# mLSTM denominators and the moments of the first norm: blocks are added on VectorE and then summed over partitions by one product each

## The chip, the core and the metric

One core of a Trainium2 chip. Its engines work side by side, each through its own list of instructions in order, and wait for one another by semaphores: TensorE (matrix products, "PE" in the profile, its loads of the stationary operand "PEld"), VectorE ("DVE"), ScalarE ("ACT"), GpSimd ("POOL") and SyncE ("SP"), which issues most transfers. The metric is device time of one execution in microseconds (us). Of the kernel before there are three timed runs: 2336.39, 2336.71 and 2338.29 us, median 2336.71.

## The reference

One inference step of a one-layer hybrid decoder for two groups of tokens: 256 tokens of a new sequence ("prompt") and 8 sequences of 8 new tokens that bring a state ("sample"), 320 tokens together. All is float32. Two mixers read one projection of the layer's input, an mLSTM with 4 heads and an HGRN2 with 8; their outputs are merged, projected, normalised, and a feed-forward block with a second norm follows. Two places matter here. The first is the mLSTM's denominator:

```python
d = jnp.exp(logd - m_t[..., None])
w_inter = jnp.exp(inter - m_t)
s = jnp.einsum('bhtk,bhsk->bhts', qc, kc) * d
num = jnp.einsum('bhts,bhsv->bhtv', s, vc) + w_inter[..., None] * jnp.einsum('bhtk,bhkv->bhtv', qc, C)
den = jnp.sum(s, axis=-1) + w_inter * jnp.einsum('bhtk,bhk->bht', qc, n)
h = num / jnp.maximum(jnp.abs(den), jnp.exp(-m_t))[..., None]
```

The second is the first of the two layer norms:

```python
x1 = _layernorm(DEEPNORM_ALPHA * x + mix, ln1_g, ln1_b)      # mean and variance over 2048 channels
hid = jnp.square(jax.nn.relu(jnp.einsum('btd,df->btf', x1, w_up)))
y = _layernorm(DEEPNORM_ALPHA * x1 + jnp.einsum('btf,fd->btd', hid, w_down), ln2_g, ln2_b)
```

## The kernel before

**The main stream.** Activations lie with channels on the partitions and the 320 tokens along a row. Every large projection is cut into 304 tiles of 128 output channels; a tile runs over 16 blocks of 128 input channels. To keep float32 accuracy at the faster float32r format, both operands are split into a high part and the rest, and each block takes three products (a "triple"): high x high, high x low, low x high. They are issued by `run_main` through the helper `mm` (L327), so that almost all products have line 327. In the profile a tile's bank is `bank`, the split weights are `wh`/`wl` (later also parts of `bb`), the split activations `xh`/`xl` (later `ra`, `rxb`, `bb`). Weights arrive by DMA into `wr`; `prep` splits half a tile at a time: ScalarE copies the high part (helper `A`, L321), VectorE subtracts (L469).

**Order.** The order on every engine is fixed when the program is built. `Sched` keeps a modelled clock for each engine and a list of chains (Python generators), each of which yields its next instruction with a cost. After every triple `pump` lets the chains issue what the model takes to be ready; a product of a chain goes into TensorE's stream between two triples, at the earliest 450 ns after the model has its inputs finished. `acq` and `rel` take and give back buffers and PSUM banks, `post` and `wait` are events between chains. On the chip semaphores hold an instruction back until its inputs are really there, and all that is behind it on its engine waits too.

**mLSTM, per head h.** `m_E` makes the decay factors in the tile `E` (512 columns, shown as `f`): columns 0 to 127 hold source block 0 against target block 0 of the prompt, 128 to 255 source block 0 against target block 1, 256 to 383 source block 1 against target block 1, and 384 to 511 the sample tokens (rows 64 to 127; the other rows and the columns between are zero). `m_S` multiplies the scores of queries and keys in (L859, L860), so that `E` holds `s`, and splits it into `sh`, `sl` (L868) and the sample's `ss` (L869). `m_num` computes the prompt's outputs. Its denominators, column sums of `E`, come first: three products of a 128 x 128 block of `E`, as the stationary operand, with a column of ones (`one`, in the tile `misc`), so each of them is one column wide. Target block 1 takes two of them, added up in PSUM. Then come the numerators (512 columns wide), and `ln_post` and `rsqrt` for the head's norm on VectorE and ScalarE (L974 to L995). `m_sample` does the sample: eight products with the old states `C` (tiles `f` and `rx`), two of `ss` with `vs`, and the denominator: the column sum of `E[:, 384:512]` and of the two halves of `qn`, which holds the query times the old normaliser, again with `one`, three products into one PSUM column. L1101 copies it to SBUF. All of that is issued between the triples of the main stream while the head's neighbours and the merge gates are projected; `sigmoid` (L1209 to L1216) turns the gates.

**Layer norm.** `ev_wo` (first norm) and `ev_dn` (second) add the residual to each of the 16 blocks `z` of 128 channels. `ln_sum` keeps two running sums on VectorE, S1 of z (L1678) and S2 of its square (L1679; the square on ScalarE), for the tiles up to 14. Then `ln_pre` multiplies S1 and S2 with a 128 x 128 block of ones (`ones`), which sums over partitions and spreads the sum to all of them; the products are 320 columns wide and stay open in PSUM. When the last block arrives, `ln_final` adds two more products, of z and of its square, to the same banks, and the statistics follow on ScalarE and VectorE (L1705 to L1713). After the first norm the products with `w_up` don't wait for the statistics; they run on z scaled by the norm's gain (`zg`, L1754), and `ev_up` applies the statistics behind them.

Of the kernel before, what the change touches and what calls it, by code (L numbers as in the profile page):

```python
# [13 lines left out]
ALU = mybir.AluOpType  # L14
# [6 lines left out]
TOK = 320  # L21
# [201 lines left out]
def wait(*evs):  # L223
    return ("wait", evs)


def acq(pool, n=1):
    return ("acq", pool, n)
# [6 lines left out]
def post(ev):  # L235
    return ("set", ev)


def act(n, psum=False, ptr=0):
    return ((61 if psum else 112) + n) / 1.2 + 93 * ptr  # L240
# [6 lines left out]
def pe_f(n, m=128):  # L247
    return max(212.0 if m == 128 else 162.0, n * 1.66)
# [35 lines left out]
class Program:  # L284
# [561 lines left out]
    def m_S(self, h):  # L846
        v, m = self.nc.vector, self.mh[h]
        if h:
            yield wait(self.mh[h - 1]["S"])
        yield wait(*m["q"], *m["k"], m["E"])  # L850
        b = yield acq(self.sbank)
        qk = m["qk"]
        for lo, n, ks, qs in ((0, 256, 0, lambda c: qk[:, c, 0:256]), (256, 128, 128, lambda c: qk[:, c, 128:256]),
                              (384, 64, 192, lambda c: by_row(qk[:, c, :], 256, False))):
            for c in range(2):
                yield ("pe", pe_f(n), lambda: self.mm(
                    b[:, lo:lo + n], qk[:, 2 + c, ks:ks + 128], qs(c), start=c == 0, stop=c == 1))
        E, Es = m["eb"], m["Es"]
        yield ("dve", dve(384, True), lambda: v.tensor_tensor(E[:, 0:384], b[:, 0:384], E[:, 0:384], ALU.mult))  # L859
        yield ("dve", dve(64, True), lambda: v.tensor_tensor(Es, b[64:128, 384:448].rearrange("p (x r) -> p x r", x=4), Es, ALU.mult))  # L860
        yield rel(self.sbank, b)
        shl = yield acq(self.shl)
        m["shl"] = shl
        sh, sl, ss = shl
        f = lambda x: x.bitcast(F32)
        yield ("act", act(384), lambda: self.A(sh, E[:, 0:384]))
        yield ("act", act(128), lambda: self.A(ss[64:128, 0:128], E[64:128, 384:512]))
        yield ("dve", dve(384), lambda: v.tensor_tensor(sl, E[:, 0:384], f(sh), ALU.subtract))  # L868
        yield ("dve", dve(128), lambda: v.tensor_tensor(ss[64:128, 128:256], E[64:128, 384:512], f(ss[64:128, 0:128]), ALU.subtract))  # L869
        yield ("act", act(256), lambda: self.A(ss[0:64], f(ss[64:128])))  # L870
        yield post(m["S"])

    def m_V(self, h):
# [123 lines left out]
    def m_num(self, h):  # L997
        v, m = self.nc.vector, self.mh[h]
        if h:
            yield wait(self.mh[h - 1]["N"])  # L1000
        yield wait(m["S"], m["Vt"])
        hb = yield acq(self.hb)
        m["hb"] = hb
        E = m["eb"]
        sh, sl, ss = m["shl"]
        vh, vl = m["vhl"][:, 0], m["vhl"][:, 1]
        db = yield acq(self.sbank)
        m["db"] = db
        one = self.one
        yield ("pe", 212, lambda: self.mm(db[:, 0:1], E[:, 0:128], one, start=True, stop=True))  # L1010
        yield ("pe", 212, lambda: self.mm(db[:, 1:2], E[:, 128:256], one, start=True, stop=False))
        yield ("pe", 212, lambda: self.mm(db[:, 1:2], E[:, 256:384], one, start=False, stop=True))
        for i in range(2):
            b = yield acq(self.sbank)
            jobs = [(c, s) for c, s in (((0, 0),), ((128, 0), (256, 1)))[i]]
            n = 0
            for c, s in jobs:
                for x, w in ((sh, vh), (sh, vl), (sl, vh)):
                    st, sp = n == 0, n == 3 * len(jobs) - 1
                    yield ("pe", pe_r(512), lambda: self.mm(b, x[:, c:c + 128], w[:, s, :], start=st, stop=sp))  # L1020
                    n += 1
            yield from self.ln_post(h, i, b, db[:, i:i + 1], hb[:, i, :], 128, True)
            yield rel(self.sbank, b)
        yield rel(self.sbank, db)
        yield post(m["N"])
# [40 lines left out]
    def m_sample(self, h):  # L1066
        nc, v, m = self.nc, self.nc.vector, self.mh[h]
        if h:
            yield wait(self.mh[h - 1]["QW"])
        yield wait(*m["q"], m["bc_"], self.rows_ev)  # L1070
        qk, bc = m["qk"], m["bc"]

        qz = yield acq(self.qz)
        qn = yield acq(self.qn)
        for c in range(2):
            qc = cap(qz, 256 * c, [[136, 2], [32, 4], [1, 8]])
            yield ("dve", dve(64), lambda: v.tensor_tensor(qc, by_token(qk[:, c, :], 256, False), by_token(bc, 640, False), ALU.mult))
            n4 = cap(self.n0[:, h, c, :], 0, [[4, 2], [1, 4], [0, 8]])
            yield ("dve", dve(64), lambda: v.tensor_tensor(by_token(qn, 128 * c, True), qc, n4, ALU.mult))
        yield post(m["QW"])  # L1080
        nb = yield acq(self.sbank)
        for k in range(2):
            yield wait(*m["parts"][8 * k:8 * k + 8])
            cbs = m["cbs"][8 * k:8 * k + 8]
            yield ("pe", PE_C, lambda: [self.mm(
                nb[32 * x:32 * x + 32, :], qz[:, 256 * c + 128 * k + 32 * x:256 * c + 128 * k + 32 * x + 32], cbs[4 * c + x],
                start=k == 0 and c == 0, stop=False, skip_group_check=True) for c in range(2) for x in range(4)])
            for c in range(2):
                self.s.spawn(self.m_update(h, 8 * k + 4 * c, cbs[4 * c:4 * c + 4]), 3)
        yield rel(self.qz, qz)  # L1090
        yield wait(m["S"], m["Vt"])
        E = m["eb"]
        ss = m["shl"][2]
        for i in range(2):
            yield ("pe", pe_r(512), lambda: self.mm(nb, ss[:, 128 * i:128 * i + 128], m["vs"], start=False, stop=i == 1, skip_group_check=True))
        db = yield acq(self.sbank)
        yield ("pe", 212, lambda: self.mm(db[:, 0:1], E[:, 384:512], self.one, start=True, stop=False))
        for c in range(2):
            yield ("pe", 212, lambda: self.mm(db[:, 0:1], qn[:, 128 * c:128 * c + 128], self.one, start=False, stop=c == 1))
        dn = yield acq(self.sm)  # L1100
        yield ("dve", 80, lambda: v.tensor_copy(dn[:, 0:1], db[:, 0:1]))  # L1101
        yield rel(self.sbank, db)
        yield rel(self.qn, qn)
        yield post(m["S0"])
        yield wait(m["N"])
        hb = m["hb"]
        yield from self.ln_post(h, 2, nb, dn[:, 0:1], hb[:, 2, :], 128, True)
        yield rel(self.sbank, nb)
        yield rel(self.sm, dn)
        for j in range(4):  # L1110
            b = yield acq(self.sbank)
            for i in range(3):
                yield ("pe", PE_T, lambda: nc.tensor.transpose(b[:, 128 * i:128 * i + 128], hb[:, i, 128 * j:128 * j + 128], self.ident))  # L1113
            jj = 4 * h + j
            o = yield acq(self.tst)
            g = self.vec[:, V_MLG + jj:V_MLG + jj + 1]
            yield ("act", act(NP_, True, 1), lambda: self.A(o[:, 0:NP_], b[:, 0:NP_], scale=g))
            yield ("act", act(64, True, 1), lambda: self.A(by_row(o, NP_, False), by_row(b, NP_, True), scale=g))
            yield rel(self.sbank, b)
            yield ("sp", 620, lambda: self.dma(self.hT[jj], o))  # L1120
            yield post(self.hT_ev[jj])
            yield wait(self.later(2500))
            yield rel(self.tst, o)
        yield rel(self.hb, hb)
        yield wait(*m["inter"])
        yield rel(self.bc, bc)
        yield wait(m["KS"])
        yield post(m["end"])
        if h == MH - 1:
            yield ("sp", 620, lambda: self.dma(self.d["n_out"][:, 0:8], self.np_o))  # L1130
            yield ("sp", 620, lambda: self.dma(self.d["n_out"][:, 8:72], self.nso_flat))
# [501 lines left out]
    def ln_add(self, n, j, z, pre):  # L1633
# [29 lines left out]
            return  # L1663
        yield from self.ln_sum(j, z)
        yield post(st["s"][j])
        if j == 14:
            self.s.spawn(self.ln_pre(n), 0)

    def ln_sum(self, j, z):
# [19 lines left out]
    def ln_final(self, n, z):  # L1689
# [3 lines left out]
        M, RS, X, T = (self.lnb[i] for i in (3, 4, 5, 6))  # L1693
        q = yield acq(self.tmp)
        t = yield ("act", act(TOK), lambda: self.A(q, z, AF.Square))
        yield wait(st["pre"])
        p1, p2 = (p[:, :TOK] for p in st["p"])
        yield ("pe", pe_f(TOK), lambda: self.mm(p1, self.ones, z, start=False, stop=True))
        yield ("pe", pe_f(TOK), lambda: self.mm(p2, self.ones, q, start=False, stop=True))
        yield rel(self.tmp, q)  # L1700
        yield post(st["fin"])
        t = yield ("act", act(TOK, True), lambda: self.A(M, p1, scale=1.0 / D))
# [217 lines left out]
```

## Time and profile before

| | |
|---|---|
| median of 3 runs | 2336.71 us |
| profiled execution, its own time | 2337.24 us |
| its span (first to last instruction) | 2335.5 us |
| TensorE busy | 2320.3 us (99%) |
| VectorE busy | 1370.3 us (59%) |
| ScalarE busy | 1049.6 us (45%) |
| transfers, mean over the span | 182 GB/s |

The profile records one execution. A group's row names line, engine, operation, output and inputs, shape, count, then busy time and mean duration of one, and the idle time before it with what ended it. A timeline's row has start, duration, engine, line, operation and, in brackets, idle time before it. A float32 product that is not float32r leaves two records. The mLSTM heads lie between about 60 and 450 us, the first norm ends near 1412 us. Durations of TensorE's records overlap, since its products are pipelined.

### The profile page before, as it was taken

What the parts mean: (1) busy time and instruction counts of PE and PEld (TensorE: products, weight loads), DVE (VectorE), ACT (ScalarE), POOL (GpSimd) and SP (SyncE); (2) the same over time, 40 slices, a digit from 0 to 9 for tenths busy, and PEclk for the clock granted to TensorE, in tenths of its full rate; (3) what the DMA queues carried; (4) which work ended last, traced back from release to release, by engine and by line L of the source; (5) the groups of instructions that cost most, each with busy time, mean ns of one, the idle gap of its engine ahead of it and who ended that gap; (6) DMA issues with size and microseconds to landing.
All of it is one profiled execution on the core that took longest, in us unless ns stands there. A gap on an engine that the chain in (4) does not pass through costs nothing.

```text
span 2335.5 us, 39111 instructions
## 1 busy us (share of the span) xinstructions
PE 2320.3 (99%) x15858; PEld 2274.2 (97%) x15858; DVE 1370.3 (59%) x2320; ACT 1049.6 (45%) x1669; POOL 13.4 (1%) x57
## 2 busy tenths in 40 slices
PE   8999999999999999999999999999999999999998
PEld 7999999999999999999999999999999999999998
DVE  5566557666766776555555767544554455445555
ACT  4444445455555465444433446532443344334434
POOL 0000000000000000000000000000000000000000
PEclk9999999999999999999999999999999999999999
DMA  5777776555555554554555644444444444444465
GB/s 207 258 269 265 256 237 227 196 183 181 181 181 175 183 195 166 181 173 170 176 171 176 221 167 142 147 153 145 149 149 151 148 147 152 150 148 146 153 226 180
DMA packets 143564, 425.03 MB, mean 182 GB/s; under 512 B 16404, under 2 KB 37780, under 8 KB 142360
## 3 DMA queue, kind: packets, MB, share of 16 engines
q1 hardware_dynamic: 142232, 416.25, 51.7%
q0 software_dynamic: 1152, 6.29, 0.8%
q8 instruction: 124, 2.03, 0.4%
q14 instruction: 56, 0.46, 0.1%
HBM read 371.57 MB, written 50.90 MB: 181 GB/s over the span
## 4 chain that ended last, share of the span: by engine, by line
PE 98%; DVE 1%; DMA 0%; ACT 0%; SPq 0%; issue 0%; DVEq 0%
PE bank L327 97%; DVE f3m L1809 0%; DVE f3m L1814 0%; DMA wr<-wt 0%; PE bank L1113 0%; PE bank L1518 0%; PE bank L887 0%; DMA f<-scr 0%; PE bank L1348 0%; SPq L330 0%; PE bank L960 0%; PE bank L1406 0%; PE bank L1353 0%; PE bank L1467 0%; PE bank L934 0%
## 5 line engine op out<-in xcount | busy, mean ns | idle before, releaser
L469 DVE TENSOR_TENSOR wl<-wr,wh 128x1024 fp32r<-128x1024 f32 (+1 forms) x430 | 525.8, 1223 | 474.2 <-ACT wh L321 468.7
L327 PE MATMUL bank<-xh,wh 128*128 128x320 f32 (+1 forms) x2432 | 793.2, 326 | 0.7 <-ACT wh L321 0.7
L327 PE MATMUL bank<-xh,wl 128*128 128x320 f32 (+1 forms) x2432 | 754.0, 310 | 0.0
L327 PE MATMUL bank<-xl,wh 128*128 128x320 f32 (+1 forms) x2432 | 752.0, 309 | 0.0
L321 ACT ACTIVATE wh<-wr 128x1024 fp32r<-128x1024 f32 (+1 forms) x430 | 453.6, 1055 | 448.0 <-PE bank L327 426.1
L327 PEld LDWEIGHTS bank<-xh,wh 128*128 128x128 f32 x2432 | 459.0, 189 | 21.1 <-issue 15.0
L327 PEld LDWEIGHTS bank<-xl,wh 128*128 128x128 f32 x2432 | 459.6, 189 | 3.7
L327 PEld LDWEIGHTS bank<-xh,wl 128*128 128x128 f32 x2432 | 458.4, 188 | 0.2 <-DVE wl L469 0.2
L469 DVE TENSOR_TENSOR bb<-wr,bb 128x1024 fp32r<-128x1024 f32 x179 | 219.3, 1225 | 234.6 <-ACT bb L321 234.5
L327 PE MATMUL bank<-xh,bb 128*128 128x322 f32 x1280 | 287.2, 311 | 0.0
L327 PE MATMUL bank<-ra,bb 128*128 128x320 f32 x1264 | 283.6, 309 | 0.0
L321 ACT ACTIVATE bb<-wr 128x1024 fp32r<-128x1024 f32 x179 | 188.8, 1055 | 207.5 <-PE bank L327 199.8
L327 PE MATMUL bank<-rxb,bb 128*128 128x320 f32 x1112 | 255.4, 309 | 0.0
L327 PE MATMUL bank<-ra,wh 128*128 128x320 f32 x892 | 249.9, 309 | 0.0
L327 PEld LDWEIGHTS bank<-xh,bb 128*128 128x128 f32 x1280 | 215.9, 188 | 0.0
L327 PEld LDWEIGHTS bank<-ra,bb 128*128 128x128 f32 x1264 | 210.7, 188 | 0.4
L327 PE MATMUL bank<-xl,bb 128*128 128x322 f32 x640 | 198.7, 310 | 0.0
L327 PEld LDWEIGHTS bank<-rxb,bb 128*128 128x128 f32 x1112 | 188.4, 188 | 0.2
L321 ACT ACTIVATE f<-f,misc 128x320 f32<-128x320 f32 x210 | 118.2, 563 | 149.5 <-DVE f L1777 137.1
L327 PE MATMUL bank<-rxb,wh 128*128 128x320 f32 x596 | 184.2, 309 | 0.0
L327 PE MATMUL bank<-rxb,wl 128*128 128x320 f32 x596 | 183.8, 308 | 0.0
L327 PEld LDWEIGHTS bank<-ra,wh 128*128 128x128 f32 x892 | 161.5, 188 | 1.1 <-DVE ra L1548 0.9
(257 smaller groups left out, 2230.6 us busy)
## 6 DMA issues: line engine op xcount, KB each, us to landing
wr<-wt SPq DMA_DIRECT2D x607, 512.0 KB, 3.3
rx<-C SPq DMA_DIRECT2D x34, 256.0 KB, 5.7
Cs<-rx SPq DMA_DIRECT2D x34, 256.0 KB, 5.0
f<-C SPq DMA_DIRECT2D x30, 256.0 KB, 4.9
Cs<-f SPq DMA_DIRECT2D x30, 256.0 KB, 4.2
vD<-ra SPq DMA_DIRECT2D x4, 1024.0 KB, 7.1
f<-S SPq DMA_DIRECT2D x8, 512.0 KB, 6.1
f3h<-S SPq DMA_DIRECT2D x8, 512.0 KB, 5.7
```

Source lines behind the costliest of these rows:

```text
L321: return self.nc.scalar.activation(out, in_, func, **kw)
L327: self.nc.tensor.matmul(*a, **kw)
L469: self.V().tensor_tensor(lo[:, c], raw[:, c], hi[:, c].bitcast(F32), ALU.subtract)
```

## The change

- `m_S` ends with one more instruction on VectorE: `E[:, 128:256]` becomes the sum of the blocks 128 to 255 and 256 to 383, after the splits have read them and ahead of the event S.
- `m_num` makes its denominators with two products, one for each target block.
- `m_sample` adds `E[:, 384:512]` and the second half of `qn` to the first half of `qn` on VectorE, and makes the denominator with one product.
- In the first norm (n = 0) `ln_pre` is not started. `ln_final` adds the last block and its square to the running sums on VectorE, takes two banks, and makes one product for each sum. The second norm (n = 1) is as before.

```diff
@@ m_S
         yield ("act", act(256), lambda: self.A(ss[0:64], f(ss[64:128])))
+
+        yield ("dve", dve(128), lambda: v.tensor_tensor(E[:, 128:256], E[:, 128:256], E[:, 256:384], ALU.add))
         yield post(m["S"])
@@ m_num
-        yield ("pe", 212, lambda: self.mm(db[:, 0:1], E[:, 0:128], one, start=True, stop=True))
-        yield ("pe", 212, lambda: self.mm(db[:, 1:2], E[:, 128:256], one, start=True, stop=False))
-        yield ("pe", 212, lambda: self.mm(db[:, 1:2], E[:, 256:384], one, start=False, stop=True))
+        for i in range(2):
+            yield ("pe", 212, lambda: self.mm(db[:, i:i + 1], E[:, 128 * i:128 * i + 128], one, start=True, stop=True))
@@ m_sample
         db = yield acq(self.sbank)
-        yield ("pe", 212, lambda: self.mm(db[:, 0:1], E[:, 384:512], self.one, start=True, stop=False))
-        for c in range(2):
-            yield ("pe", 212, lambda: self.mm(db[:, 0:1], qn[:, 128 * c:128 * c + 128], self.one, start=False, stop=c == 1))
+
+        q0 = qn[:, 0:128]
+        yield ("dve", dve(128), lambda: v.tensor_tensor(q0, q0, E[:, 384:512], ALU.add))
+        yield ("dve", dve(128), lambda: v.tensor_tensor(q0, q0, qn[:, 128:256], ALU.add))
+        yield ("pe", 212, lambda: self.mm(db[:, 0:1], q0, self.one, start=True, stop=True))
@@ ln_add
-        if j == 14:
+        if j == 14 and n:
             self.s.spawn(self.ln_pre(n), 0)
@@ ln_final
-        yield wait(st["pre"])
+        if n:
+            yield wait(st["pre"])
+        else:
+            S1, S2 = self.lnb[0], self.lnb[1]
+            yield ("dve", dve(TOK), lambda: v.tensor_tensor(S1, S1, z, ALU.add), (t - act(TOK) - LAT,))
+            yield ("dve", dve(TOK), lambda: v.tensor_tensor(q, S2, q, ALU.add), (t,))
+            st["p"] = yield acq(self.sbank, 2)
         p1, p2 = (p[:, :TOK] for p in st["p"])
-        yield ("pe", pe_f(TOK), lambda: self.mm(p1, self.ones, z, start=False, stop=True))
-        yield ("pe", pe_f(TOK), lambda: self.mm(p2, self.ones, q, start=False, stop=True))
+        yield ("pe", pe_f(TOK), lambda: self.mm(p1, self.ones, z if n else S1, start=n == 0, stop=True))
+        yield ("pe", pe_f(TOK), lambda: self.mm(p2, self.ones, q, start=n == 0, stop=True))
```

## Prediction

> **What bounds the kernel now.** I read the page first (parts 1, 2 and 4), then what TensorE waited for, then busy time by stretch.
>
> ```profile
> span 2335.5 us, 39111 instructions
> PE 2320.3 (99%) x15858; PEld 2274.2 (97%) x15858; DVE 1370.3 (59%) x2320; ACT 1049.6 (45%) x1669; POOL 13.4 (1%) x57
> ...
> PEclk9999999999999999999999999999999999999999
> ...
> PE 98%; DVE 1%; DMA 0%; ACT 0%; SPq 0%; issue 0%; DVEq 0%
> ```
>
> ```profile
> PE bank L327 <- DVE ra L670: 4.3, 1, 4.3
> PE bank L327 <- ACT xh L321: 2.7, 1, 2.7
> PE bank L327 <- ACT wh L321: 0.7, 1, 0.7
> PE bank L327 <- DVE ra L891: 0.5, 1, 0.5
> PE bank L327 <- DVE xl L665: 0.3, 1, 0.3
> ```
>
> ```profile
> 150.00:200.00 50.00, 50.00 (x346) 45.25 (x345) 29.59 (x58) 21.28 (x37) 0.00 (x0) 1.00 0.82 300
> 1400.00:1450.00 50.00, 50.00 (x336) 49.68 (x335) 34.99 (x58) 30.35 (x52) 0.00 (x0) 1.00 0.42 143
> ```
>
> TensorE is busy 2320.3 of 2335.5 us and makes 98% of the chain that ended last. Its recorded waits come to 8.5 us in all, and only the 0.5 us behind L891 falls after the first tile. Both stages that the change touches (mLSTM heads, first norm) have TensorE busy for every microsecond (third column of the stretches), at clock 1.00, while VectorE is busy 59% and 70% (29.59 and 34.99 of 50). So an instruction taken from TensorE's stream should shorten the run by what it adds to the spacing of that stream, and VectorE's work costs nothing as long as no product has to wait for it.
>
> A busy TensorE is not proof of a dense one, so I take prices from start-to-start distances and not from durations. In the rows below, three matmuls of L327 (xh,wh / xl,wh / xh,wl, a triple) start within 0.44 us, although each lasts 0.31.
>
> **What is removed.** Twelve one-column products (per head one of three in `m_num` and two of three in `m_sample`) and two 320-column products with `ones` (those of `ln_pre` for the first norm). As the two programs are built, the stream holds 15,502 matmuls before and 15,488 after: 14 fewer, and nothing else has gone. That rules out the rival that the change doesn't do what it says.
>
> The price of a one-column product, from head 1's last sample product in order of time (columns: start, duration):
>
> ```profile
> 191.36 0.31 PE L327 MATMUL bank<-xh,wl 128*128 128x320 f32 x1
> ...
> 191.80 0.31 PE L327 MATMUL bank<-xh,wl 128*128 128x320 f32 x1
> 191.95 0.28 PE L327 MATMUL bank<-misc,f 128*128 128x1 f32 x2
> 192.09 0.40 PE L327 MATMUL bank<-xh,wh 128*128 128x320 f32 x1
> ...
> 192.47 0.31 PE L327 MATMUL bank<-xh,wl 128*128 128x320 f32 x1
> ```
>
> Without the product the third matmul of a triple follows the last triple's third after 191.80 - 191.36 = 0.44 us; with it, after 192.47 - 191.80 = 0.67. The product costs 0.23. Twelve: 2.76 us. Its stationary operand, the block that is summed, is loaded for it alone:
>
> ```profile
> 191.80 0.34 PEld L327 LDWEIGHTS bank<-misc,f 128*128 128x128 f32 x2
> ```
>
> The page TensorE: Matmul & The Clock Gate of the Trainium skill (section Back-to-back issue gap) speaks against the change: it gives a matmul of 1 to 64 columns some 25 ns. With two records a product, twelve would save an estimated 12 x 2 x 0.025 = 0.6 us, and the sum below would be 1.7 instead of 3.86. The trace does not agree: 0.23 us is added, nine times 25 ns, and the load of the block is in it.
>
> The price of a product with `ones`, same reading, first norm:
>
> ```profile
> 1404.08 0.31 PE L327 MATMUL bank<-xh,wl 128*128 128x322 f32 x1
> 1404.23 0.70 PE L327 MATMUL bank<-f3m,ones 128*128 128x320 f32 x2
> 1404.52 0.55 PE L327 MATMUL bank<-xh,wh 128*128 128x322 f32 x1
> 1404.91 0.31 PE L327 MATMUL bank<-xl,wh 128*128 128x322 f32 x1
> 1405.07 0.31 PE L327 MATMUL bank<-xh,wl 128*128 128x322 f32 x1
> ```
>
> 1405.07 - 1404.08 = 0.99, less 0.44: 0.55 us. Two: 1.10. Removed in all: 3.86 us.
>
> An upper bound is the busy time of the groups:
>
> ```profile
> L327 PE MATMUL bank<-misc,f 128*128 128x1 f32 x48 | 6.6, 208 | 0.0
> L327 PE MATMUL bank<-f,ones 128*128 128x320 f32 x16 | 5.6, 431 | 0.0
> L327 PE MATMUL bank<-f3m,ones 128*128 128x320 f32 x4 | 1.4, 432 | 0.0
> ```
>
> Two records are one product, so 6.6/24 = 0.275 each, and 7.0/10 = 0.70 each with `ones`: 3.3 + 1.4 = 4.7 us. It counts overlapped time twice, so I take the spacing, 3.86.
>
> **What is added.** Fourteen VectorE adds: four 128x128 in `m_S`, eight in `m_sample`, two 128x320 in `ln_final`. Nearest rows (same operation and shape):
>
> ```profile
> 84.42 0.29 DVE L915 TENSOR_TENSOR f<-f 128x128 fp32r<-128x128 f32 x1
> 1394.89 0.49 DVE L1678 TENSOR_TENSOR f<-f,f3m 128x320 f32<-128x320 f32 x1
> ```
>
> 12 x 0.29 + 2 x 0.49 = 4.5 us on an engine that idles 2335.5 - 1370.3 = 965 us. I cost it at nothing: what hides it is the time in which VectorE waits for ScalarE before splitting weights, 468.7 us in 398 waits (`DVE wl L469 <- ACT wh L321`, row below). If that cover were gone it would be 4.5 us. What counts is the new wait: the remaining product now needs its adds finished, and behind it on TensorE's queue stand the weight matmuls of the main stream, on which everything waits.
>
> ```profile
> DVE wl L469 <- ACT wh L321: 468.7, 398, 4.8
> ```
>
> Adds in `m_S`, one a head: in head 1 it stands before the sigmoid's L1215, so it ends by about 179.33 + 0.29 = 179.6. TensorE's first denominator product is built three triples (1.3 us) behind its old place, after 180.5. Slack 0.9: nothing; heads 2 and 3 are built alike.
>
> ```profile
> 179.33 0.49 DVE L1215 SCALAR_TENSOR_TENSOR f<-f 128x320 f32<-128x320 f32 x1
> ```
>
> ```profile
> 179.22 0.28 PE L327 MATMUL bank<-misc,f 128*128 128x1 f32 x2
> ```
>
> First norm: z is ready at 1402.97 and its square at 1403.54 (rows below), the sums 0.5 us after each, and the two products are built one triple (0.44) later than before, after 1404.08 and 1405.51, with the weight split of 1404.97 built behind both adds. Slack 1 us and more: nothing. The two removed products precede z, so the chain of the norm is no later than it was.
>
> ```profile
> 1402.49 0.48 DVE L1736 TENSOR_TENSOR f3m<-f,bank 128x320 f32<-128x320 f32 x1
> ...
> 1403.07 0.47 ACT L321 ACTIVATE f<-f3m 128x320 f32<-128x320 f32 x1 [1.75 <-DVE f3m L1736]
> ...
> 1404.97 1.22 DVE L469 TENSOR_TENSOR wl<-wr,wh 128x1024 fp32r<-128x1024 f32 x1 [2.00 <-ACT wh L321]
> ```
>
> Adds in `m_sample`, heads 1 to 3, is the one tight place. They are built right behind L989 of `rsqrt`, and the product stays at the place of the second of the old three, the one at 191.95, whose weight load began with the matmul of 191.80.
>
> ```profile
> 184.81 1.06 ACT L321 ACTIVATE wh<-wr 128x1024 fp32r<-128x1024 f32 x1 [3.81 <-PE bank L327]
> ...
> 189.08 0.69 ACT L321 ACTIVATE f<-bank,misc 128x512 f32<-128x512 f32 x1 [1.67 <-DVE misc L976]
> ```
>
> ```profile
> 190.75 0.15 DVE L989 TENSOR_SCALAR misc<-misc 128x1 f32<-128x1 f32 x1
> 191.41 0.16 DVE L992 TENSOR_TENSOR misc<-misc 128x1 f32<-128x1 f32 x1 [0.50 <-ACT misc L321]
> ...
> 192.65 1.23 DVE L469 TENSOR_TENSOR wl<-wr,wh 128x1024 fp32r<-128x1024 f32 x1 [0.70 <-ACT wh L321]
> ```
>
> L989 ends at 190.90; two adds of 0.29 with gaps of 0.04 end at 191.56. The product's load falls 0.23 earlier than 191.80, since the first sample product is gone: 191.57. (The head's removed `m_num` product moves both sides: this VectorE chain hangs on the ScalarE copy at 184.81, which waited for TensorE.) With about 0.04 from end to release, TensorE stands some 0.05 us per head, 0.15 in three. Bounds: nothing, or, if VectorE keeps its old times (0.23 more) and the add in `m_S` pushes its chain too (0.29 and a gap), about 0.58 a head, 1.7 us. I take 0.15, as the copy's 3.81 us of waiting ties the chain to TensorE. Head 0 is built otherwise: its adds stand behind L982 and end at 107.13 + 0.66 = 107.8, its product one triple behind the old one of 108.21 and one product (0.23) earlier, 108.4: nothing.
>
> ```profile
> 106.58 0.55 DVE L982 TENSOR_SCALAR f<-f,misc 128x512 f32<-128x512 f32 x1
> ```
>
> ```profile
> 108.21 0.28 PE L327 MATMUL bank<-misc,f 128*128 128x1 f32 x2
> ```
>
>  Order elsewhere: a weight split and a few small copies change places on VectorE; the small ones are then late by up to 1.2 us, and the splits are not.
>
> **Sum.** -3.86 + 0.15 = -3.7 us. The profiled execution took 2337.24 (span 2335.5), 0.5 above the median 2336.71 of the runs shown (2336.39 to 2338.29); from the median: 2333.0 us, -0.16%. A measurement of this kernel tells about 0.2% (4.7 us) from no change, so 2332.0 and below counts as faster.
>
> **Rivals.**
> 1. The durations and not the spacings are what the stream loses: 4.7 us, 2332.0. For it: TensorE's third column is full. Against: the neighbours start while the product lasts.
> 2. VectorE is late in heads 1 to 3: 0.58 x 3 = 1.7, so 2336.7 - 3.86 + 1.7 = 2334.6. For it: the margin is 0.01 us. Against: the tie at 184.81.
> 3. One-column products are free inside the stream, so only the norm's 1.1 us go: 2335.6. Against: 0.67 beside 0.44.
> 4. Slower: the sample adds fall behind a weight split on VectorE. Then each head's product waits for the 0.70 of idle, the 1.23 of the split and 0.6 of adds, 2.5 us, four times 10: 2336.7 - 3.86 + 10 = 2342.9. It decides from 3.86/4 = 0.97 us a head. For it: VectorE takes its work in the order built, and the next split stands close behind. Against: as built, the split stands behind the adds in all four heads.
>
> **How the numbers follow.** Forecast 0.60, rival 1 0.18, rival 2 0.15, rival 3 0.04, rival 4 0.03. Faster by over 0.2%: rival 1, 0.18. Slower: rival 4, 0.03. Within: 0.79. The range goes from just below rival 1 (2331.8) past rival 2, with half a microsecond for the spread of the runs, to 2335.2; the unknown costs (gain 3.86 to 4.7, wait 0 to 1.7) lie inside.
>
> **What would show it.** TensorE still 98 to 99% busy with 28 fewer records; the misc,f group at half its count and about 3.3 us; no ones product before the last tile of w_out ends; a wait of TensorE for VectorE of at most 0.1 us at the sample product of heads 1 to 3 (a third matmul 0.67 us after the last confirms the forecast, 0.9 and more rival 2, about 3 rival 4). VectorE up by 4.5 us. Stretches after 1450 us should match those of before, shifted by 3.7 us; a longer stretch there would make the forecast wrong in a way none of these cases holds.

## The result, and the profile after

The changed kernel takes 2333.33 us (median of 20 runs, 2332.39 to 2335.28), the kernel before 2337.65 in the runs beside it (median of 20, 2336.09 to 2339.91). The ratio is 0.9982 with a 95% interval of 0.9975 to 0.9988: 4.3 us less, by the interval 2.8 to 5.8.

First the page of the profile after (parts 1, 2 and 4):

```profile
span 2331.2 us, 39059 instructions
PE 2317.2 (99%) x15830; PEld 2271.0 (97%) x15830; DVE 1372.8 (59%) x2334; ACT 1049.6 (45%) x1669; POOL 13.4 (1%) x57
...
PEclk9999999999999999999999999999999999999999
...
PE 98%; DVE 1%; DMA 0%; ACT 0%; SPq 0%; issue 0%; DVEq 0%
```

Then TensorE's waits and the two stretches (columns as before: stretch, length, TensorE, its loads, VectorE, ScalarE, GpSimd, granted clock):

```profile
PE bank L327 <- DVE ra L670: 4.3, 1, 4.3
PE bank L327 <- ACT xh L321: 1.6, 1, 1.6
PE bank L327 <- ACT wh L321: 1.0, 1, 1.0
PE bank L327 <- DVE xl L665: 0.3, 1, 0.3
```

```profile
150.00:200.00 50.00, 50.00 (x342) 44.95 (x342) 29.50 (x62) 21.90 (x37) 0.00 (x0) 1.00 0.86 299
1395.70:1445.70 50.00, 50.00 (x336) 49.68 (x335) 36.06 (x61) 30.24 (x52) 0.00 (x0) 1.00 0.42 148
```

The picture is the same, four microseconds shorter: TensorE makes 98% of the closing chain, has 28 records fewer, and no wait for the new adds is listed. What the change did to the stream is seen by looking up one and the same product of the main stream in the two timelines:

| point in the main stream | start before | start after | earlier by |
|---|---|---|---|
| first tile | 40.09 | 40.04 | 0.05 |
| behind a VectorE split of the mLSTM values (L891) | 66.67 | 66.23 | 0.44 |
| behind head 0 | 114.25 | 113.16 | 1.09 |
| inside head 0's output transposes | 164.70 | 163.83 | 0.87 |
| behind head 1 | 201.78 | 200.13 | 1.65 |
| behind head 2 | 288.64 | 286.20 | 2.44 |
| behind head 3 | 375.52 | 372.29 | 3.23 |
| first product of w_up | 1400.21 | 1395.91 | 4.30 |
| late in the last w_down pass | 2280.45 | 2276.16 | 4.29 |

The heads give 0.65 + 0.78 + 0.79 + 0.79 = 3.01 us and the first norm 1.07, together 4.08. The rest, 0.05 + 0.39 - 0.22, lies where both programs have the same instructions: the one execution before waited 0.5 us behind L891, the one after 0.28 us in another place, where a weight load waited for L917. From 1400 us on nothing moves any more.

Where a wait was possible, at the sample product of head 1, the timelines of TensorE, of its loads and of VectorE after the change read:

```profile
190.25 0.31 PE L327 MATMUL bank<-xl,wh 128*128 128x320 f32 x1
190.40 0.31 PE L327 MATMUL bank<-xh,wl 128*128 128x320 f32 x1
190.54 0.28 PE L327 MATMUL bank<-misc,f 128*128 128x1 f32 x2
190.68 0.40 PE L327 MATMUL bank<-xh,wh 128*128 128x320 f32 x1
190.92 0.31 PE L327 MATMUL bank<-xl,wh 128*128 128x320 f32 x1
191.07 0.31 PE L327 MATMUL bank<-xh,wl 128*128 128x320 f32 x1
```

```profile
190.40 0.34 PEld L327 LDWEIGHTS bank<-misc,f 128*128 128x128 f32 x2
```

```profile
189.61 0.15 DVE L991 TENSOR_SCALAR misc<-misc 128x1 f32<-128x1 f32 x1
189.68 0.28 DVE L1100 TENSOR_TENSOR f<-f 128x128 f32<-128x128 f32 x1
189.99 0.29 DVE L1101 TENSOR_TENSOR f<-f 128x128 f32<-128x128 f32 x1
```

The second add ends at 190.28, the product's load begins at 190.40, and the third matmul of a triple comes 0.67 us after the last one (191.07 - 190.40): no wait, with 0.12 us to spare. In heads 2 and 3 that distance is 0.67 too. ScalarE's copy, by which the prediction ties this chain to TensorE, began at 184.81 before; it is 1.15 us earlier now, and the matmuls around it 1.14:

```profile
183.66 1.06 ACT L321 ACTIVATE wh<-wr 128x1024 fp32r<-128x1024 f32 x1 [3.78 <-PE bank L327]
```

In the first norm the adds and the product stand like this:

```profile
1398.71 0.49 DVE L1703 TENSOR_TENSOR f<-f,f3m 128x320 f32<-128x320 f32 x1
1399.27 0.49 DVE L1704 TENSOR_TENSOR f<-f 128x320 f32<-128x320 f32 x1
```

```profile
1400.37 0.70 PE L327 MATMUL bank<-f,ones 128*128 128x320 f32 x2
...
1401.81 0.70 PE L327 MATMUL bank<-f,ones 128*128 128x320 f32 x2
```

The sums are ready at 1399.20 and 1399.76, over a microsecond ahead of the products at 1400.37 and 1401.81. The groups have shrunk as counted:

```profile
L327 PE MATMUL bank<-f,ones 128*128 128x320 f32 x14 | 4.9, 434 | 0.0
L327 PE MATMUL bank<-misc,f 128*128 128x1 f32 x24 | 3.3, 208 | 0.0
L327 PE MATMUL bank<-f3m,ones 128*128 128x320 f32 x2 | 0.7, 432 | 0.0
```

### The profile page after: what moved, and what is told of

The parts are those of the page before. It is cut to its first block, busy times and chain, and to the rows that moved or that the text cites. A ratio compares the mean times of both kernels' runs of the same rounds, so it can differ in the third digit from the quotient of the medians.

```text
span 2331.2 us, 39059 instructions
## 1 busy us (share of the span) xinstructions
PE 2317.2 (99%) x15830; PEld 2271.0 (97%) x15830; DVE 1372.8 (59%) x2334; ACT 1049.6 (45%) x1669; POOL 13.4 (1%) x57
## 4 chain that ended last, share of the span: by engine, by line
PE 98%; DVE 1%; DMA 0%; ACT 0%; SPq 0%; issue 0%; DVEq 0%
PE bank L327 97%; DVE f3m L1818 0%; DVE f3m L1823 0%; PE bank L1116 0%; PE bank L889 0%; PE bank L1521 0%; DMA wr<-wt 0%; PE bank L1351 0%; SPq L330 0%; PE bank L962 0%; PE bank L1356 0%; PE bank L1409 0%; PE bank L1470 0%; PE bank L936 0%; ACT f L321 0%
```

## The experiments

Each kernel was timed in five rounds beside the kernel before on the same chip, and the ratios are against it (2337.68 us beside experiments 1 to 4, 2337.79 beside 5 to 7). A difference from the changed kernel is taken from its 2333.33 us above, which come from other rounds, with 2337.65 beside them. "In the stream" means the same product of the main stream looked up in two timelines, as in the table above; that is one execution of each kernel. The intervals of experiments 1 to 4 include no change, so the stream decides there.

**1. The denominators of the prompt alone.** Against the kernel before: the add at the end of `m_S`, and two products for three in `m_num`.

```diff
+        yield ("dve", dve(128), lambda: v.tensor_tensor(E[:, 128:256], E[:, 128:256], E[:, 256:384], ALU.add))
...
-        yield ("pe", 212, lambda: self.mm(db[:, 0:1], E[:, 0:128], one, start=True, stop=True))
-        yield ("pe", 212, lambda: self.mm(db[:, 1:2], E[:, 128:256], one, start=True, stop=False))
-        yield ("pe", 212, lambda: self.mm(db[:, 1:2], E[:, 256:384], one, start=False, stop=True))
+        for i in range(2):
+            yield ("pe", 212, lambda: self.mm(db[:, i:i + 1], E[:, 128 * i:128 * i + 128], one, start=True, stop=True))
```

> The add in m_S and the two denominator products in m_num alone; m_sample and the first norm as before. Theory (a product costs what it adds to the spacing of TensorE's stream, the add costs nothing): four products gone, 4 x 0.23 = 0.9 us less than before, and in the stream each head after its denominators stands 0.23 us earlier than the head before it. Rival (durations, 0.275 a product by the group's busy time): 1.1 us. Rival (one-column products are free inside the stream): no change.

Measured: 2336.53 us beside 2337.68, ratio 0.9993 (0.9984 to 1.0002), 1.15 us less. In the stream heads 1, 2 and 3 give 0.33, 0.34 and 0.34 us (from 0.11 to 0.44, 0.78, 1.12), not 0.23. Head 0 gives 0.15 (from -0.04 at 90 us, behind a wait of 0.9 us for L893 in this execution, to 0.11 at 150). So the part has its gain; heads 1 to 3 have 0.11 us each more than the product's price, and head 0 has 0.08 less. Experiment 4 shows that the surplus doesn't come from the product.

**2. The denominators of the sample alone.** Against the kernel before: two adds and one product for three products in `m_sample`.

```diff
-        yield ("pe", 212, lambda: self.mm(db[:, 0:1], E[:, 384:512], self.one, start=True, stop=False))
-        for c in range(2):
-            yield ("pe", 212, lambda: self.mm(db[:, 0:1], qn[:, 128 * c:128 * c + 128], self.one, start=False, stop=c == 1))
+        q0 = qn[:, 0:128]
+        yield ("dve", dve(128), lambda: v.tensor_tensor(q0, q0, E[:, 384:512], ALU.add))
+        yield ("dve", dve(128), lambda: v.tensor_tensor(q0, q0, qn[:, 128:256], ALU.add))
+        yield ("pe", 212, lambda: self.mm(db[:, 0:1], q0, self.one, start=True, stop=True))
```

> The two sample adds and the single sample product alone; the rest as before. Theory: eight products gone, 8 x 0.23 = 1.8 us less than before, 0.46 a head in the stream, and the one product left has no wait of TensorE in front of it, since the adds end about 0.1 us before its load begins. Rival (VectorE late): up to 0.58 us of waiting a head in heads 1 to 3, so 0.1 to 1.8 us less than before. Rival (durations): 2.2 us.

Measured: 2335.97 us, ratio 0.9992 (0.9983 to 1.0001), 1.7 us less. In the stream 0.46 us in head 0 and 0.49 in each of heads 1 to 3 (0.38, 0.87, 1.36, 1.86), and no wait for the adds is listed. Two products at 0.23 are 0.46: the theory's price, and none of the 0.58 of the rival that has VectorE late.

**3. The first norm alone.** Against the kernel before: `ln_add` and `ln_final` of the change, the heads as before.

```diff
-        if j == 14:
+        if j == 14 and n:
             self.s.spawn(self.ln_pre(n), 0)
...
+            yield ("dve", dve(TOK), lambda: v.tensor_tensor(S1, S1, z, ALU.add), (t - act(TOK) - LAT,))
+            yield ("dve", dve(TOK), lambda: v.tensor_tensor(q, S2, q, ALU.add), (t,))
...
+        yield ("pe", pe_f(TOK), lambda: self.mm(p1, self.ones, z if n else S1, start=n == 0, stop=True))
+        yield ("pe", pe_f(TOK), lambda: self.mm(p2, self.ones, q, start=n == 0, stop=True))
```

> The first norm's part alone; the denominators as before. Theory: two products with ones gone, 2 x 0.55 = 1.1 us less than before, all of it inside the last tile of w_out. Rival (durations): 1.4 us. Rival (the adds hold back the two products that are left): less than 1.1 us, with a wait in front of them.

Measured: 2336.52 us, ratio 0.9994 (0.9985 to 1.0002), 1.2 us less. In the stream it is 0.24 us ahead up to the last tile of w_out and 1.32 at the first product of w_up: 1.08 us, near the 1.1 of the theory and not the 1.4 of the durations. No wait is listed in front of the two products that are left. The three parts give 1.16, 1.94 and 1.08 us in the stream, 4.18 together; the change gave 4.08.

**4. The adds alone.** Against the kernel before: the change's adds write to areas that nothing reads, `sc` (one of 128 columns in the heads, one of 320 in the norm), and all products stay as they were.

```diff
+        yield ("dve", dve(128), lambda: v.tensor_tensor(sc, E[:, 128:256], E[:, 256:384], ALU.add))
...
+        yield ("dve", dve(128), lambda: v.tensor_tensor(sc, qn[:, 0:128], E[:, 384:512], ALU.add))
+        yield ("dve", dve(128), lambda: v.tensor_tensor(sc, sc, qn[:, 128:256], ALU.add))
...
+            yield ("dve", dve(TOK), lambda: v.tensor_tensor(sc, self.lnb[0], z, ALU.add), (t - act(TOK) - LAT,))
+            yield ("dve", dve(TOK), lambda: v.tensor_tensor(sc, self.lnb[1], q, ALU.add), (t,))
```

> The kernel before with the fourteen adds put in at the same places, into a scratch area that nothing reads; all products as before. Theory: the adds lie in VectorE's idle time, so TensorE's stream and the time are those of before within 0.2 us, and VectorE is busy 4.1 to 4.5 us longer. Rival (they delay the weight splits or the release of banks): up to 4.5 us more than before.

Measured: 2337.25 us beside 2337.68, ratio 0.9998 (0.9989 to 1.0007). In the stream nothing is lost in heads 1 to 3 and at the two adds of the first norm, so the adds cost nothing there. VectorE was busy 1374.0 us against 1370.3, 3.7 longer. Head 0 lost 0.53 us in this execution (from 1.16 us ahead at 90 us to 0.63 at 150). It went into the eight products with the old states: from the matmul ahead of them to the one behind them 2.67 us pass, 2.09 in the kernel before, and a weight load among them waited for a transfer of `C`:

```profile
102.51 0.14 PEld L327 LDWEIGHTS bank<-f 128*32 128x32 f32 x2 [0.44 <-DMA f<-C]
```

The changed kernel makes the same adds, and there the eight products take 2.09 us. So this looks like a late transfer of one execution and not like a price of the adds; why it was late stays open.

Also unexpected: in the stream each of heads 1 to 3 stands a little earlier than the one before it, 0.10, 0.12 and 0.13 us (0.63, 0.73, 0.85, 0.98), though not one product is missing. The add at the end of `m_S` moves the head's denominators and numerators by a triple or more, so the new order is the likely place. The same tenth shows in experiment 1, and experiment 2, which has no add in `m_S`, has 0.03. How the order makes it isn't settled: the same triples take 0.44 instead of 0.45 us at several places, which is the resolution of the rows.

**5. Late adds.** Against the changed kernel. The order on TensorE is that of the changed kernel; three VectorE instructions that serve nothing stand between the two sample adds.

```diff
-        yield ("dve", dve(128), lambda: v.tensor_tensor(q0, q0, qn[:, 128:256], ALU.add))
+        sc = self.f1[:, 9984:10240]
+        yield ("dve", dve(128), lambda: [*(v.tensor_tensor(sc, qn, qn, ALU.add) for _ in range(3)),
+                                         v.tensor_tensor(q0, q0, qn[:, 128:256], ALU.add)])
```

> The changed kernel with three more VectorE instructions (128 x 256, about 0.41 us each, into a scratch area that nothing reads) between the two sample adds of each head; the order on TensorE is that of the changed kernel. In the changed kernel the adds end 0.12 us before the product's load in head 1 and 0.66 us before it in head 0. Theory (a late add holds the whole stream, one for one): 1.3 - 0.12 us in each of heads 1 to 3 and 1.3 - 0.66 in head 0, 4.2 us more than the changed kernel, which is about the time of the kernel before. Rival (TensorE makes it up, or the wait is covered): no more than 0.5 us above the changed kernel.

Measured: 2338.22 us beside 2337.79, ratio 1.0002 (0.9993 to 1.0011): the whole gain is gone, 4.9 us above the changed kernel's median. TensorE's waits (total, times, longest) and the place in head 1:

```profile
PE bank L327 <- DVE f L1103: 3.5, 4, 1.0
```

```profile
189.91 0.28 DVE L1100 TENSOR_TENSOR f<-f 128x128 f32<-128x128 f32 x1
190.23 1.35 DVE L1102 TENSOR_TENSOR f<-f 128x256 f32<-128x256 f32 x3
191.61 0.29 DVE L1103 TENSOR_TENSOR f<-f 128x128 f32<-128x128 f32 x1
```

```profile
190.63 0.31 PE L327 MATMUL bank<-xh,wl 128*128 128x320 f32 x1
191.96 0.38 PE L327 MATMUL bank<-misc,f 128*128 128x1 f32 x2 [1.02 <-DVE f L1103]
192.20 0.39 PE L327 MATMUL bank<-xh,wh 128*128 128x320 f32 x1
```

The product starts 1.33 us after the matmul ahead of it where 0.14 was enough in the changed kernel (190.54 - 190.40). In the stream heads 1, 2 and 3 lose 1.29, 1.28 and 1.28 us against the changed kernel (-0.23, -1.52, -2.80, -4.08), a tenth more than expected; head 0 loses 0.70 where 0.64 was expected. Nothing of it is made up later. The listed wait of 1.02 is shorter than the loss, since it counts only the time in which no record was running. At its end this execution stands 4.84 us behind that of the changed kernel, and 0.68 of it is a wait in the first norm that has nothing to do with the edit (see the last section).

**6. More products.** Against the changed kernel: eleven sample products a head instead of one; ten results are not read.

```diff
-        yield ("pe", 212, lambda: self.mm(db[:, 0:1], q0, self.one, start=True, stop=True))
+        for i in range(11):
+            yield ("pe", 212, lambda: self.mm(db[:, i:i + 1], q0, self.one, start=True, stop=True))
```

> The changed kernel with the sample's one-column product made eleven times a head instead of once, into eleven columns of the same bank, of which one is read. Theory: 40 more products at 0.23 us, 9.2 us more than the changed kernel. Rival (durations): 0.275 each by the group's busy time, 11.0 us more. Rival (almost free inside the stream; 25 ns a record by the Trainium skill's page TensorE: Matmul & The Clock Gate, section Back-to-back issue gap, an estimate): 2.0 us more.

Measured: 2342.59 us beside 2337.79, ratio 1.0022 (1.0013 to 1.0031), 9.26 us above the changed kernel's median, 0.23 for each of the 40. In the stream the end stands 9.27 us later, 0.34 of which lay ahead of head 0 already: 8.93, or 0.22 each. The group's row:

```profile
L327 PE MATMUL bank<-misc,f 128*128 128x1 f32 x104 | 14.4, 208 | 0.0
```

Its busy time rose from 3.3 to 14.4, by 11.1 us, and the run by 9.3: the busy time of a group overstates what the stream loses by a fifth. Two records of 208 ns are 0.42 us a product, nearly double. The page TensorE: Matmul & The Clock Gate of the Trainium skill (section Back-to-back issue gap) has some 25 ns for a matmul of 1 to 64 columns, which for 40 products of two records would be an estimated 40 x 2 x 0.025 = 2.0 us. The run doesn't agree: 9.3. The section itself says that its formula for a single matmul counts too little at small sizes, as the weight load is not in it; here every record of a product has a load of its own.

**7. Both norms.** Against the changed kernel: the second norm is made like the first.

```diff
-        if j == 14 and n:
-            self.s.spawn(self.ln_pre(n), 0)
...
-        if n:
-            yield wait(st["pre"])
-        else:
-            S1, S2 = self.lnb[0], self.lnb[1]
+        S1, S2 = self.lnb[0], self.lnb[1]
...
-        yield ("pe", pe_f(TOK), lambda: self.mm(p1, self.ones, z if n else S1, start=n == 0, stop=True))
-        yield ("pe", pe_f(TOK), lambda: self.mm(p2, self.ones, q, start=n == 0, stop=True))
+        yield ("pe", pe_f(TOK), lambda: self.mm(p1, self.ones, S1, start=True, stop=True))
+        yield ("pe", pe_f(TOK), lambda: self.mm(p2, self.ones, q, start=True, stop=True))
```

> The changed kernel with the second norm made like the first: ln_pre is never started, the last block and its square are added on VectorE. Theory: two products with ones fewer before the end, 1.1 us off TensorE's stream; at the end the two adds (0.49 us each) stand in the closing chain, but the second product there followed the first by 0.54 us anyway, so the chain is 0 to 0.5 us later. 0.6 to 1.1 us less than the changed kernel. Rival (the adds and their waits in the closing chain cost what the products gave): no change or slower.

Measured: 2332.48 us beside 2337.79, ratio 0.9977 (0.9968 to 0.9986), and 0.85 us below the changed kernel's median; the two intervals overlap, so the order of these two isn't proved by the times. In the stream the two products are worth 1.08 us (1.36 behind the changed kernel at 2290 us, 0.28 behind it at 2302). Its second norm in the timeline, and under it the same place of the kernel before:

```profile
2305.89 0.49 DVE L1796 TENSOR_TENSOR f3m<-f3m,bank 128x320 f32<-128x320 f32 x1 [5.06 <-PE bank L327]
2306.41 0.49 DVE L1698 TENSOR_TENSOR f<-f,f3m 128x320 f32<-128x320 f32 x1
2306.47 0.47 ACT L321 ACTIVATE f<-f3m 128x320 f32<-128x320 f32 x1 [6.57 <-DVE f3m L1796]
2306.97 0.49 DVE L1699 TENSOR_TENSOR f<-f 128x320 f32<-128x320 f32 x1
2307.08 1.25 PE L327 MATMUL bank<-f,ones 128*128 128x320 f32 x4
```

```profile
2309.89 0.49 DVE L1792 TENSOR_TENSOR f3m<-f3m,bank 128x320 f32<-128x320 f32 x1 [6.14 <-PE bank L327]
...
2311.08 0.70 PE L327 MATMUL bank<-f3m,ones 128*128 128x320 f32 x2
...
2311.62 0.70 PE L327 MATMUL bank<-f,ones 128*128 128x320 f32 x2
```

The first add runs beside ScalarE's square, and the second ends at 2307.46. The products follow one another from 2307.08, 1.19 us after the last block's residual add began (2305.89); before it was 2311.08 - 2309.89 = 1.19 too. The last of them ends at 2308.33, 2.44 us after that add began; before it was 2312.32 - 2309.89 = 2.43. So the adds cost the closing chain nothing. Of the kernels run, this one has the lowest median.

## Why the prediction was right

It gave 2333.0 us, a range of 2331.8 to 2335.2, and no difference by over 0.2% as the likeliest; 2333.33 was measured, 0.18% less than before. That the two medians lie so near is in part luck: the forecast took 3.7 us off a median of three runs, 2336.71, and 4.3 us came off 2337.65. That the difference stays under 0.2% was near as well: its interval reaches from 0.12 to 0.25%.

- *TensorE bounds the kernel, and what leaves its stream leaves the time.* Right: 4.08 us left the stream at the places of the change, 4.3 left the median.
- *A one-column product costs 0.23 us, twelve 2.76.* Right in price: experiment 6 gives 0.23 over 40 products by the times, 0.22 in the stream. The comparison "nine times 25 ns" was not fair, since a product is two records and the 25 ns of the Trainium skill (page TensorE: Matmul & The Clock Gate, section Back-to-back issue gap) are for one matmul; by record it is between four and five times. The heads gave 3.01 us, 0.25 more than twelve such products. That is not a mis-sized product: experiment 4 shows 0.10 to 0.13 us a head in heads 1 to 3 without any product removed. The prediction had no term for a change of order on TensorE, which is its likely place; the cause stays open.
- *A product with ones costs 0.55 us, two 1.10.* Right: 1.07 in the change, 1.08 alone, 1.08 for the second norm.
- *Fourteen adds cost nothing.* Right, as far as experiment 4 goes. Their sum was right too: in the changed kernel the groups of the five new lines have 1.1, 1.1, 1.2, 0.5 and 0.5 us, together 4.4. But VectorE's busy time rose by 2.5 us and not by 4.5, and by 3.7 in experiment 4. Busy time counts an overlap once, and the first sample add of head 1 began 0.08 us before the recorded end of L991; why the two kernels differ stays open, and no forecast of time hangs on it.
- *0.15 us of waiting at the sample products.* Mis-sized: there is none. The tie that the prediction rested on holds: ScalarE's copy, at 184.81 before, is at 183.66 after, 1.15 earlier and so with the stream. The step that failed is the spacing of the adds, counted as 0.29 with gaps of 0.04 behind the end of the instruction ahead. The first one started 0.07 after L991 had begun, before its recorded end, so the margin was 0.12 us and not 0.01.
- *Rival 1 (durations, 4.7 us)* came nearer to the median than its mechanism deserves. Experiment 6 rules it out for the one-column products, 9.3 us and not 11, and the norm's 1.08 us, not 1.4, for those with ones.
- *Rival 2 (VectorE late, 1.7 us)* didn't occur, in the change or in experiment 2.
- *Rival 3 (free products)* is ruled out by experiment 6 as well.
- *Rival 4 (adds late, the gain lost from 0.97 us a head)* did not occur, but its mechanism is real: experiment 5 made the second add about 1.3 us later and lost 1.28 to 1.29 us in each of heads 1 to 3, and the kernel was no faster than before.

## What to carry to other kernels

Where one engine is busy from end to end, price an instruction by the distance between its neighbours' starts with and without it, not by its duration or its group's busy time: 0.23 us here, against 0.275 by the group and 0.42 by durations. Work moved to an engine with idle time cost nothing here where it ended before the dense engine came to the instruction that needs it; look up that margin (0.12 us here) before the sum, as in experiment 5 every microsecond beyond it was lost one for one. On a dense engine pieces of 1 us can be shown by looking up the same instruction in two timelines where their run times can't, between two points that have no wait of a single execution between them.

## What the runs showed that was not expected

Waits of TensorE that come and go from one execution to the next are as large as the parts of this change. In five of the nine profiles (experiments 1, 2, 4, 5 and 7) the stream lost 0.3 to 0.7 us at the first norm's first product with ones, that of `ln_add` for the centre; in the others it didn't. The rows of ScalarE, VectorE and TensorE in experiment 1:

```profile
1314.33 1.06 ACT L321 ACTIVATE bb<-wr 128x1024 fp32r<-128x1024 f32 x1 [2.61 <-DMA wr<-wt]
```

```profile
1315.42 1.23 DVE L469 TENSOR_TENSOR bb<-wr,bb 128x1024 fp32r<-128x1024 f32 x1 [1.75 <-ACT bb L321]
1316.56 0.48 DVE L1644 TENSOR_TENSOR f<-f,f3m 128x320 f32<-128x320 f32 x1
```

```profile
1316.36 0.31 PE L327 MATMUL bank<-rxb,wl 128*128 128x320 f32 x1
1317.10 0.81 PE L327 MATMUL bank<-f,ones 128*128 128x320 f32 x2 [0.43 <-DVE f L1644]
```

A transfer of weights landed late (2.61 us of waiting on ScalarE): in the kernel before, whose stream is 1.12 us later here, the same copy began at 1314.16 and had waited for TensorE and not for a transfer. So the weight split came late on VectorE; the running sum S1, of which the product is made, was queued behind it, and TensorE stood until it was done. In the stream that is 0.7 us (1.12 ahead of the kernel before, then 0.42). It is rival 4's mechanism at another place, in instructions that the change did not touch. Why the transfer lands late in some executions stays open.
